# Five edits to a one-core hybrid attention/convolution layer kernel: q's norm factor in the exponential's scale, the side bank in halves, late quarters of q, the gate's division, the first and the last block

## The chip, the cores and the metric

One core of one Trainium2 chip runs the whole layer in one launch. The metric is device time in microseconds. The kernel before was timed three times: 932.99, 933.21 and 934.81 us, median 933.21 us. Lower is better.

## The reference

One sequence of T = 512 tokens, model width D = 2048, one layer. The products are float32, and the kernel must reproduce them closely, which is why it splits each operand (below).

```python
h = rms_norm(x, norm_gain)
z = h @ w_in                                  # 2048 x 6656
q, k, v, g_attn, c_b, c_c, c_h, g_conv = split(z)
q = partial_rope(rms_norm(q, q_norm_gain))    # 16 heads of 64
k = partial_rope(rms_norm(k, k_norm_gain))    # 4 heads of 64
# sliding window of 128, blocks of 128, a learned sink per head
scores = q @ k.T * HEAD_DIM ** -0.5           # masked
m = max(max(scores), sink)
e = exp(scores - m)
probs = e / (sum(e) + exp(sink - m))
y_attn = (probs @ v) * silu(g_attn)
y_conv = c_b * conv3(c_c * c_h) * silu(g_conv)
x = x + concat(y_attn, y_conv) @ w_out
gate = sigmoid(rms_norm(x, ple_gate_norm_gain) @ w_ple_gate + b_ple_gate)
x = x + gate * rms_norm(p @ w_ple_proj, ple_norm_gain)
```

## The kernel before

**Products.** Every float32 operand is split into two parts of a shorter format, a high and a low one (`halves`, L199 a cast on ACT, L200 a subtraction on DVE), and each product is three matmuls: high by high, low by high, high by low. Weights arrive by DMA (`wx`, `wy`, `ws`, `raw`), their parts are `wh` and `wl`; the parts of the activations are `hsh` and `hsl`, and sums of them, used by a seven-product scheme, are called `form`.

**Head.** K and V are projected first, in eight chunks c of two k each (L482 to L504). Inside the loop the next chunk's weights are split, then the next two blocks of x are multiplied by the norm's gain and split (`split_x`, L427 to L431), then some forms are made. For blocks 0 and 1 the split reads x directly (L427, L428), and x itself is rescaled in place right after (L429); from block 2 on, x is rescaled (L431) and then split.

**Groups.** Then come nine groups of 28 steps (`run_step`). A step is twelve matmuls of 128x512 at L241, 2.72 us. Ahead of its matmuls a step makes the weight sums needed four steps on and splits the weight needed two steps on; behind them come the jobs entered with `soon(after, s, ...)`. The split has three buffers, so it cannot run ahead by more than that. Group 0 makes q, in quarters: `qs[t, n]` holds token blocks 2t and 2t+1 of column half n. Quarters (0,1) and (1,1) are joined in steps 17 to 22, (0,0) and (1,0) only at its end. Groups 1 to 8 make the gate of the convolution, the convolution, the gate of the attention (group 4), the output projection (5 and 6) and the gate of the embeddings (7 and 8).

**Norms.** The norm of x is not applied ahead of the projection. Its factor per token, `rx_tok`, and the head norms are applied behind it: `head_sums` squares a quarter (ACT) and sums it per head (DVE L548); `head_rstd` multiplies by the square of the token factor (L552), scales (L300) and raises to the power -1/2 on POOL (L305); `times_token` (L556) multiplies by the token factor again; `scale_q` multiplies q by the result (L579, 128x512 each) and `rope` turns it (L407 to L409). `rb` (L709) is a 128x512 copy of `rx2_tok`, the square of that factor (the profile prints both as rx_tok), which four transposes on PE (L734) turn into rows for K; ACT copies them out of PSUM to `rx` (L735).

**Attention.** It runs beside seven GEMM tiles of the convolution (`gemm_tile`, L700). After every six matmuls of a tile (1.36 us) a tick lets due work in. The sixteen units (four heads of one K/V head, one block of 128 queries) start at tick 13 + 34u//15: `turn_q` three ticks earlier (two transposes of q into the side bank `psm`, L777, evicted into `st` at L781 and L782), then the scores (L790, L791), the mask and the maximum (L796, on DVE, four per unit, result `negm`), the exponentials (L801, ACT), the sums (L805 to L808), the transposes of the probabilities (L816) five ticks after the scores, their split into `pth` and `ptl`, and the product with the values (L826, L827) at seven ticks.

**Group 4.** z, the gate's projection, goes through silu (L992) and is divided by the softmax's sums: `normalise` (L1079) multiplies eight pieces of 128x64 by one column of `rs` each, on ACT, per call. Then it is transposed and multiplied by the attention's output (`times`, L1090).

**Last steps.** The embedding gate's last blocks: `whole` (L1231) adds up z, a sigmoid follows (L1298), then the factor of e (L1246) and x (L1300).

**What sets the order.** On every engine the instructions stand in one queue and start in the order of the queue. PE's order is the order of the code throughout. In the head, in group 0 and in the groups behind the attention the other queues follow the code too; in the attention phase a scheduler orders ACT, DVE and POOL by their readiness, and can put an instruction of the second phase into the end of group 0.

Of the kernel before, what the change touches and what calls it, by code (L numbers as in the profile page):

```python
# [15 lines left out]
P = 128  # L16
# [19 lines left out]
def hymba_layer(ctx: ExitStack, tc: tile.TileContext, io):  # L36
# [177 lines left out]
    def run_step(s, forms):  # L214
# [21 lines left out]
        def products(t, f=f, c=c, wh=wh, wl=wl, first=first, last=last):  # L236
            for i in range(2):
                _, h, l = forms[2 * c + i][f]
                h, l = (a[:, t * P : (t + 1) * P] for a in (h, l))
                for n, (a, w) in enumerate(((h, wh), (l, wh), (h, wl))):  # L240
                    nc.tensor.matmul(  # L241
                        ps[t], a, w[:, i], start=start and first and i == 0 and n == 0,
                        stop=last and i == 1 and n == 2, skip_group_check=not start,
                    )
# [4 lines left out]
        elif s == len(steps) - 1:  # L249
# [4 lines left out]
            products(1)  # L254
# [161 lines left out]
    def split_w(c, i=None):  # L416
        if i is None:
            kv_split.append(new_split())
            halves(*kv_split[c], kv_raw[c])
        else:  # L420
            halves(*(w[:, i] for w in kv_split[c]), kv_raw[c][:, i])

    def split_x(k):
        x, g = xpair[k // 2][:, k % 2], norm_g[:, k : k + 1]
        h, l = (hsp.tile([P, T], F32R, tag="h", name="hs" + n) for n in "hl")
        if k < 2:
            nc.scalar.activation(h, x, AF.Copy, scale=g)  # L427
            stt(l, x, g, f32(h), op0=ALU.mult, op1=ALU.subtract)  # L428
            nc.scalar.activation(x, x, AF.Copy, scale=g)  # L429
        else:  # L430
            nc.scalar.activation(x, x, AF.Copy, scale=g)  # L431
# [46 lines left out]
    kv_split.append(new_split())  # L478
# [3 lines left out]
    for c in range(8):  # L482
        if c > 1:
            form63(c - 2) if c - 2 < 6 else None
        if c < 7:
            split_w(c + 1)
            split_x(2 * c + 2)
            split_x(2 * c + 3)
        else:
            prepare(1)  # L490
        form_sums(c)
# [76 lines left out]
    def finish_q(t, n, junk):  # L568
        ms = small.tile([P, 2, 8], F32, name="msq", bufs=4)
        blocks = slice(2 * t, 2 * t + 2)  # L570
        z = q_of(t, n)

        def squares(b):
            head_sums(z[:, b], ms[:, b], junk("sqq"))

        def scale():
            times_token(ms, tok["x"][:, blocks])
            for b in range(2):
                tt(z[:, b], z[:, b], ms[:, b].unsqueeze(2).broadcast_to([P, 8, HD]), op=ALU.mult)  # L579

        return squares, lambda: head_rstd(ms, rx2_tok[:, blocks]), scale, lambda: rope(z, 0, blocks, mtile)
# [45 lines left out]
    q_then = {}  # L627

    def square_q(t, n, b, junk):
        if b == 0:  # L630
            squares, *q_then[t, n] = finish_q(t, n, junk)
            q_then[t, n].append(squares)
        q_then[t, n][3](b)

    for t in range(2):
        for b in range(2):
            soon(after, 21 + t + b, square_q, t, 1, b, itile)
        soon(after, 23 + t, lambda t=t: q_then[t, 1][0]())
# [30 lines left out]
    ps_m = second.enter_context(tc.tile_pool(name="ps_m", bufs=1, space=PSUM, side="right", reuse_waits="tile"))  # L669

# [798 lines left out]
```

## Time and profile before

| what | value |
| --- | --- |
| median of three runs | 933.21 us |
| the profiled execution's own time | 934.14 us |
| its span | 932.4 us |
| mean granted clock of PE | 0.995 of full speed |
| DVE busy | 731.0 us, 78% |
| ACT busy | 543.2 us, 58% |
| POOL busy | 150.5 us, 16% |
| DMA moved | 189.83 MB, 204 GB/s on average |

An engine's row says how long it had work under way; the waits of an engine say how long it stood still and which engine's result ended that. Of an instruction's row, the first number is its start, the second its duration, and a wait before it stands in brackets with what ended it. Matmuls overlap, so the distance between two starts (0.23 us for 128x512) and not the duration is what one costs.

### The profile page before, as it was taken

The page shows a single profiled execution, that of the slowest core. Times are in us where ns is not written, and L with a number is a line of the kernel's source. Part 1 is how long each engine was busy: PE and PEld are TensorE (multiplying, and loading weights), DVE is VectorE, ACT ScalarE, POOL GpSimd, SP SyncE. Part 2 cuts the span into 40 slices and gives each one's busy share as a digit, 9 for nine tenths or more (in the row PEclk, how much of TensorE's full clock was granted, in tenths as well). Part 3 has the DMA queues.
Part 4 walks back from the last instruction along what each step waited for, and adds up shares of the span by engine and source line. Part 5 has one row for each costly group of instructions (what it writes and reads, how often), then busy time and mean ns, then how long its engine had stood idle before and what let it go on. Part 6 is the DMA issues. An engine that isn't in the chain of part 4 may idle for free.

```text
span 932.4 us, 12106 instructions
## 1 busy us (share of the span) xinstructions
PE 912.5 (98%) x4202; PEld 755.6 (81%) x4202; DVE 731.0 (78%) x1064; ACT 543.2 (58%) x903; POOL 150.5 (16%) x200
## 2 busy tenths in 40 slices
PE   8999999899999999999999999999999999999997
PEld 7888878778888888888888888778888888888885
DVE  5878897888865777776768678878868696999778
ACT  6767856667862443545345357665657566665452
POOL 4232032323231001000100110011120112001100
PEclk9999999999999999999999999999999999999999
DMA  8999536434458768327725988675996895578747
GB/s 296 361 297 313 184 113 231 168 76 91 102 118 271 282 206 225 90 97 224 198 89 169 283 231 243 207 177 166 280 340 176 226 301 136 136 238 270 181 135 214
DMA packets 69085, 189.83 MB, mean 204 GB/s; under 512 B 8096, under 2 KB 14560, under 8 KB 69024
## 3 DMA queue, kind: packets, MB, share of 16 engines
q1 hardware_dynamic: 47520, 131.09, 40.5%
q0 software_dynamic: 21360, 57.96, 28.0%
q8 instruction: 33, 0.54, 0.2%
q14 instruction: 28, 0.23, 0.1%
q10 hardware_dynamic: 144, 0.01, 0.0%
HBM read 159.67 MB, written 29.36 MB: 203 GB/s over the span
## 4 chain that ended last, share of the span: by engine, by line
PE 64%; DVE 3%; ACT 1%; DMA 1%; issue 1%; SPq 0%; DVEq 0%
PE psp L241 57%; PE pst L241 4%; PE pst L986 1%; DMA e<-e 1%; PE pst L1346 1%; PE psg L700 1%; DVE wl L200 1%; ACT z L1079 1%; DVE form L200 0%; DVE wy L189 0%; ACT z L992 0%; DVE raw L1090 0%; ACT wh L199 0%; DVE z L323 0%; ACT form L199 0%
## 5 line engine op out<-in xcount | busy, mean ns | idle before, releaser
L241 PE MATMUL psp<-wh,form 128*128 128x512 f32 x1280 | 396.3, 391 | 2.1 <-ACT wh L199 2.1
L241 PEld LDWEIGHTS psp<-wh,form 128*128 128x128 f32 x1280 | 240.0, 188 | 51.7 <-ACT wh L199 2.5
L241 PE MATMUL psp<-wl,form 128*128 128x512 f32 x640 | 249.8, 390 | 0.0
L200 DVE TENSOR_TENSOR wl<-wy,wh 128x1024 fp32r<-128x1024 f32 x108 | 131.7, 1222 | 54.6 <-ACT wh L199 53.8
L199 ACT CAST wh<-wy 128x1024 fp32r<-128x1024 f32 x108 | 113.3, 1051 | 94.4 <-PE psp L241 70.8
L241 PEld LDWEIGHTS psp<-wl,form 128*128 128x128 f32 x640 | 120.4, 188 | 25.8 <-DVE wl L200 0.8
L200 DVE TENSOR_TENSOR wl<-wx,wh 128x1024 fp32r<-128x1024 f32 x72 | 88.0, 1223 | 51.1 <-ACT wh L199 51.0
L241 PE MATMUL psp<-wl,hsh 128*128 128x512 f32 x304 | 118.7, 390 | 2.0 <-DVE wl L200 2.0
L199 ACT CAST wh<-ws 128x1024 fp32r<-128x1024 f32 x72 | 75.9, 1054 | 74.0 <-PE psp L241 53.3
L241 PE MATMUL psp<-wh,hsh 128*128 128x512 f32 x304 | 118.8, 391 | 0.0
L241 PE MATMUL psp<-wh,hsl 128*128 128x512 f32 x304 | 118.3, 389 | 0.0
L199 ACT CAST wh<-wx 128x1024 fp32r<-128x1024 f32 x72 | 75.7, 1052 | 73.0 <-PE psp L241 51.1
L200 DVE TENSOR_TENSOR wl<-ws,wh 128x1024 fp32r<-128x1024 f32 x72 | 88.1, 1223 | 29.0 <-ACT wh L199 28.8
L189 DVE TENSOR_TENSOR wy<-wy,ws 128x1024 f32<-128x1024 f32 x72 | 87.7, 1218 | 0.0
L241 PEld LDWEIGHTS psp<-wl,hsh 128*128 128x128 f32 x304 | 57.1, 188 | 14.9 <-DVE wl L200 2.9
L241 PEld LDWEIGHTS psp<-wh,hsl 128*128 128x128 f32 x304 | 57.1, 188 | 11.8
L241 PEld LDWEIGHTS psp<-wh,hsh 128*128 128x128 f32 x304 | 57.1, 188 | 11.7 <-ACT wh L199 0.2
L700 PE MATMUL psg<-hsh,wh 128*128 128x512 f32 x112 | 46.7, 417 | 0.0
L200 DVE TENSOR_TENSOR wl<-raw,wh 128x1024 fp32r<-128x1024 f32 (+1 forms) x29 | 34.4, 1187 | 15.2 <-ACT wh L199 15.0
L169 POOL DMA_DIRECT2D wy<-in_w_mid x16 | 14.0, 874 | 199.2 <-DVE wy L189 108.7
L700 PE MATMUL psg<-hsl,wh 128*128 128x512 f32 x112 | 44.2, 395 | 0.0
L700 PE MATMUL psg<-hsh,wl 128*128 128x512 f32 x112 | 44.2, 394 | 0.0
(218 smaller groups left out, 1324.9 us busy)
## 6 DMA issues: line engine op xcount, KB each, us to landing
ws<-in_w_mid SPq DMA_DIRECT2D x40, 512.0 KB, 4.5
wx<-in_w_mid SPq DMA_DIRECT2D x24, 512.0 KB, 3.5
wy<-in_w_mid SPq DMA_DIRECT2D x20, 512.0 KB, 6.1
h<-form POOLq DMA_DIRECT2D x32, 256.0 KB, 5.8
wy<-in_w_mid POOLq DMA_DIRECT2D x16, 512.0 KB, 8.3
raw<-in_w_in SPq DMA_DIRECT2D x16, 512.0 KB, 3.6
wx<-in_w_out SPq DMA_DIRECT2D x16, 512.0 KB, 6.6
ws<-in_w_out SPq DMA_DIRECT2D x16, 512.0 KB, 5.4
```

What stands on the lines that cost most here:

```text
L169: nc.gpsimd.dma_start(t, w[n, r, j, c], accum_op=ALU.add)
L189: tt(y, y, got[g, "s1" if f == 6 else "s0", c], op=ALU.add)
L199: nc.scalar.copy(h, src)
L200: tt(l, src, f32(h), op=ALU.subtract)
L241: nc.tensor.matmul(ps[t], a, w[:, i], start=start and first and i == 0 and n == 0, stop=last and i == 1 and n == 2, skip_group_check=not s ...
L700: nc.tensor.matmul(ps, w[:, k % 8], a, start=k == 0 and n == 0, stop=k == KT - 1 and n == 2)
L986: nc.tensor.transpose(pt[:, b], quads[b // 2][:, b % 2, f * P : (f + 1) * P], ident)
L1079: nc.scalar.activation(z, z, AF.Copy, scale=rs[:, 2 * t + b, 8 * n + i : 8 * n + i + 1])
L1346: nc.tensor.matmul(ps, w[:, k % 8], a, start=k == 0 and n == 0, stop=k == KT - 1 and n == 2)
```

## The change

- **Head.** `split_x` splits blocks 0 to 3 from x directly, and the rescaling of x is its own function, called later in the loop: blocks 0 and 1 behind chunk 0's splits, 2 and 3 behind chunk 1's. Chunk 1's weight is split in two halves, each followed by one block of x, and the very first weight half is cast on DVE.
- **rx's rows.** `rb` and its four transposes move from the attention phase (at tick 2) to behind step 25 of group 0; the copy out of PSUM follows the start of the second phase.
- **q's head norms.** `finish_q` falls into `square_q`, `rstd_q` and `rope_q`. The quarter is no longer multiplied (eight operations of 128x512 go); instead the factor enters the softmax. The maximum is taken over the unscaled scores, two new operations of 128x4 turn it into `negm` (L809, L810), and the exponential reads the factor as its scale. `times_token` now follows `head_rstd` at once. In group 0, `rstd_q` of quarters (0,1) and (1,1) stands behind steps 24 and 25, where `head_rstd` stood behind 23 and 24.
- **Late quarters.** The squares of (0,0) and (1,0) move from ticks 13 and 14 to ticks 19 to 22, their factors from 14 and 15 to 21 and 23, their rope from 19 and 20 to 24 and 26.
- **Side bank.** `psm` is one tile of two halves; `turn_q` takes them in turn, and K's four transposes go two and two.
- **Spacing.** Units start at 13 + 36u//15.
- **Group 4.** `normalise` takes four pieces at a time, at steps 18 to 24, 28 and 29; the first half of quarter (0,0) and the last quarter go through DVE (`normalise_wide`); and these jobs are entered behind those that make the forms.
- **Last step.** Its second half of matmuls goes in two halves of columns (twelve of 128x256 for six of 128x512), and the sigmoid of a piece follows its `whole`.

DVE at the end of group 0, before, between the subtractions for steps 25 and 26 and the copy of `rb` (`msq_1205` and `msq_1233` are the sums of squares of quarters (0,1) and (1,1), `msk` is K's, `ptsl` the low part of the layer's embeddings; `wl_1265` belongs to step 26, `wl_1288` to step 27):

```order
L556 TENSOR_TENSOR msk_715<-msk_715,r_x_1202 128x16
L757 SCALAR_TENSOR_TENSOR vv_1421<-kv_713,r_x_1202,vv_1421 128x4x64
L300 TENSOR_SCALAR msq_1205<-msq_1205 128x16
L548 TENSOR_REDUCE msq_1233<-sqq_1257 128x8
L200 TENSOR_TENSOR wl_1265<-wy_576,wh_1264 128x1024
L552 TENSOR_TENSOR msq_1233<-msq_1233,rx2_tok_716 128x16
L200 TENSOR_TENSOR ptsl_1373<-pt_1262,ptsh_1372 128x1024
L300 TENSOR_SCALAR msq_1233<-msq_1233 128x16
L200 TENSOR_TENSOR wl_1288<-wy_579,wh_1287 128x1024
L323 TENSOR_TENSOR z_786<-z_786,psp_1077 128x1024
L200 TENSOR_TENSOR wl_1317<-raw_1260,wh_1316 128x1024
L709 COPY rb_1376<-rx2_tok_716 128x512
```

The same place after, from `ptsl` on, with the quarters' sums now `msq_1207` and `msq_1235`; `wl_1288` belongs to step 27, and the subtractions for steps 25 and 26 stand ahead of the first row. L570 is `times_token`, which reads what POOL has raised to the power behind L301:

```order
L200 TENSOR_TENSOR ptsl_1385<-pt_1261,ptsh_1384 128x1024
L301 TENSOR_SCALAR msq_1207<-msq_1207 128x16
L570 TENSOR_TENSOR msk_717<-msk_717,r_x_1204 128x16
L765 SCALAR_TENSOR_TENSOR vv_1425<-kv_715,r_x_1204,vv_1425 128x4x64
L570 TENSOR_TENSOR msq_1207<-msq_1207,r_x_1204 128x16
L200 TENSOR_TENSOR wl_1288<-wy_581,wh_1287 128x1024
L566 TENSOR_TENSOR msq_1235<-msq_1235,rx2_tok_718 128x16
L576 TENSOR_TENSOR kv_713<-kv_713,msk_717 128x256
L301 TENSOR_SCALAR msq_1235<-msq_1235 128x16
L576 TENSOR_TENSOR kv_714<-kv_714,msk_717 128x256
L570 TENSOR_TENSOR msq_1235<-msq_1235,r_x_1204 128x16
L650 COPY rb_1307<-rx2_tok_718 128x512
```

Before, nothing in this stretch reads the powers of `msq`; after, two rows do, each behind its own L301, and the second of them is the row ahead of the copy of `rb`.

On PE, the transposes of `rb` stood among the GEMM's matmuls, before:

```order
L700 MATMUL psg_1426<-hsl_263,wh_1316 128x512
L700 MATMUL psg_1426<-hsh_262,wl_1317 128x512
L734 MATMUL psm_1445<-ident_211,rb_1376 128x128 x4
L700 MATMUL psg_1426<-hsh_310,wh_1316 128x512
L700 MATMUL psg_1426<-hsl_311,wh_1316 128x512
L700 MATMUL psg_1426<-hsh_310,wl_1317 128x512
```

and after they stand between the last matmul of step 25 and the first of step 26 of group 0:

```order
L241 MATMUL psp_1079<-wh_1240,hsl_624 128x512
L241 MATMUL psp_1079<-wl_1241,hsh_623 128x512
L653 MATMUL pst_1309<-ident_211,rb_1307 128x128 x4
L241 MATMUL psp_723<-wh_1263,hsh_434 128x512
L241 MATMUL psp_723<-wh_1263,hsl_435 128x512
L241 MATMUL psp_723<-wl_1264,hsh_434 128x512
```

They have moved ahead of 24 matmuls of group 0 and 12 of the GEMM.

On ACT in group 4, from the cast of the weight for step 23 (`wy`), before:

```order
L199 CAST wh_5483<-wy_4818 128x1024
L992 ACTIVATE z_5132<-z_5132,r_x_1202 128x512 x2
L1079 ACTIVATE z_5132<-z_5132,rs_1423 128x64 x8
L199 CAST form_5511<-raw_5328 128x256
L199 CAST form_5514<-g_5479 128x256
L199 CAST wh_5523<-wy_4841 128x1024
L1079 ACTIVATE z_5132<-z_5132,rs_1423 128x64 x8
```

and after:

```order
L199 CAST wh_5490<-wy_4829 128x1024
L199 CAST form_5508<-raw_5339 128x256
L199 CAST form_5511<-g_5482 128x256
L1003 ACTIVATE z_5143<-z_5143,r_x_1204 128x512 x2
L1079 ACTIVATE z_5319<-z_5319,rs_1428 128x64 x4
L199 CAST wh_5526<-wy_4852 128x1024
```

The two forms have moved ahead of the silu and of the division, and four pieces of the division instead of eight stand ahead of the next weight's cast.

The diff, cut to its core:

```diff
@@ run_step
-        def products(t, f=f, c=c, wh=wh, wl=wl, first=first, last=last):
+        def products(t, f=f, c=c, wh=wh, wl=wl, first=first, last=last, cols=slice(0, T)):
...
-            products(1)
+            for half in range(2):
+                products(1, cols=slice(half * 2 * P, (half + 1) * 2 * P))
@@ head
+    def scale_x(k):
+        x = xpair[k // 2][:, k % 2]
+        nc.scalar.activation(x, x, AF.Copy, scale=norm_g[:, k : k + 1])
...
-        if k < 2:
+        if k < 4:
             nc.scalar.activation(h, x, AF.Copy, scale=g)
             stt(l, x, g, f32(h), op0=ALU.mult, op1=ALU.subtract)
-            nc.scalar.activation(x, x, AF.Copy, scale=g)
...
-            split_w(c + 1)
-            split_x(2 * c + 2)
-            split_x(2 * c + 3)
+            if c:
+                split_w(c + 1)
+            for i in range(2):
+                if c == 0:
+                    split_w(1, i)
+                split_x(2 * c + 2 + i)
...
+        if c < 2:
+            for i in range(2):
+                scale_x(2 * c + i)
@@ group 0
+    def rstd_q(t, n):
+        head_rstd(rq[t, n], rx2_tok[:, blocks])
+        times_token(rq[t, n], tok["x"][:, blocks])
...
-        soon(after, 23 + t, lambda t=t: q_then[t, 1][0]())
+        soon(after, 24 + t, rstd_q, t, 1)
+    def rx2_rows():
+        rb = itile("rb").rearrange("p (b t) -> p b t", t=P)
+        nc.vector.tensor_copy(rb, rx2_tok.unsqueeze(2).broadcast_to([P, NB, P]))
+        rows_ps.append(ps_t.tile([P, T], F32, name="pst"))
+        for b in range(NB):
+            nc.tensor.transpose(rows_ps[0][:, b * P : (b + 1) * P], rb[:, b, :], ident)
+
+    soon(after, 25, rx2_rows)
@@ attention phase
+    psm = ps_m.tile([P, 2, 2 * P], F32, name="psm")
...
-            at(13 + t, lambda t=t, b=b: square_q(t, 0, b, mtile))
-        at(14 + t, lambda t=t: q_then[t, 0][0]())
-        at(19 + t, lambda t=t: scale_q(t, 0))
+            at(19 + 2 * t + b, lambda t=t, b=b: square_q(t, 0, b, mtile))
+        at(21 + 2 * t, lambda t=t: rstd_q(t, 0))
+        at(24 + 2 * t, lambda t=t: rope_q(t, 0))
...
-            pt = ps_m.tile([P, T], F32, name="psm")[:, : 2 * P].rearrange("p (f t) -> p f t", t=P)
+            pt = psm[:, turns_done[0] % 2].rearrange("p (f t) -> p f t", t=P)
...
-                    t[:, r, lo:], sc[r // 2][:, r % 2, lo:], mask[:, lo:], -(HD**-0.5), nsink[:, h : h + 1],
-                    ALU.add, ALU.min, negm[:, r : r + 1],
+                    t[:, r, lo:], sc[r // 2][:, r % 2, lo:], mask[:, lo:], HD**-0.5, NEG,
+                    ALU.add, ALU.max, negm[:, r : r + 1],
                 )
+            tt(negm, negm, r_q, op=ALU.mult)
+            stt(negm, negm, -1.0, nsink[:, 4 * j : 4 * j + 4], op0=ALU.mult, op1=ALU.min)
...
-                    t[:, r, lo:], t[:, r, lo:], AF.Exp, scale=-1.0, bias=negm[:, r : r + 1],
+                    t[:, r, lo:], t[:, r, lo:], AF.Exp, scale=r_q[:, r : r + 1], bias=negm[:, r : r + 1],
...
-        attention(j, n, 13 + 34 * u // 15)
+        attention(j, n, 13 + 36 * u // 15)
@@ attn_group
-        soon(after, s0 + 21, lambda: normalise(1, 1, 0))
-        soon(after, s0 + 22, lambda: normalise(1, 1, 1))
...
+        for t, n, b, h, s in (
+            (0, 1, 0, 0, 18), (0, 1, 1, 0, 19), (0, 1, 0, 1, 20), (0, 1, 1, 1, 21),
+            (1, 1, 0, 0, 22), (1, 1, 1, 0, 22), (1, 1, 0, 1, 23), (1, 1, 1, 1, 24), (0, 0, 0, 1, 28), (0, 0, 1, 1, 29),
+        ):
+            soon(after, s0 + s, normalise, t, n, b, h)
@@ gate_group
             for c in cols:
                 whole(1, 0, b, c)
+                nc.scalar.activation(q[1, 0][:, b, c], q[1, 0][:, b, c], AF.Sigmoid)
             for c in cols:
-                piece(1, 0, b, c)
+                piece(1, 0, b, c, True)
```

98 lines of the change are left out of this document (43 added, 55 removed).

## The prediction

> **What bounds the kernel now.** I read the page's row of PE first, then the list of what PE waited for, then its granted clock around the two longest waits.
>
> ```profile
> PE 912.5 (98%) x4202; PEld 755.6 (81%) x4202; DVE 731.0 (78%) x1064; ACT 543.2 (58%) x903; POOL 150.5 (16%) x200
> ```
>
> PE has work under way in 98% of the span, and the change takes almost no matmul away. So it can win only what PE loses by standing still or by a lowered clock, and lose only by making PE stand still elsewhere.
>
> ```profile
> PE psm L777 <- DVE st L782: 2.6, 3, 1.0
> PE pss L790 <- DVE negm L796: 2.5, 1, 2.5
> PE psp L241 <- ACT wh L199: 2.1, 1, 2.1
> PE psp L241 <- DVE wl L200: 2.0, 2, 1.9
> PE psm L740 <- ACT rx L735: 1.4, 1, 1.4
> PE psp L501 <- ACT hsh L199: 1.3, 1, 1.3
> ...
> PE pso L827 <- DVE ptl L200: 0.5, 1, 0.5
> ```
>
> Columns: total us, number, longest. The first, second and last rows belong to the attention phase, the third and fourth to group 4, the fifth to the start of the second phase, the sixth to the head: the edits aim at every one of them. A wait also costs what the clock loses behind it; of three stretches (busy times by engine, then PEclk, then DMA share and GB/s):
>
> ```profile
> 186.00:190.00 4.00, 3.99 (x16) 3.31 (x15) 3.81 (x12) 1.67 (x9) 0.00 (x0) 0.57 0.16 57
> 596.00:600.00 4.00, 3.76 (x15) 2.79 (x16) 4.00 (x7) 3.58 (x5) 0.00 (x0) 1.00 1.02 289
> 613.00:618.00 5.00, 4.96 (x14) 3.58 (x15) 3.37 (x4) 5.00 (x13) 0.00 (x0) 0.67 1.05 271
> ```
>
> Behind the wait of 2.54 us the clock was 0.57 for 4 us, 4 x 0.43 = 1.7 us lost; behind the 2.09 us wait 5 x 0.33 = 1.65 us; behind the 1.87 us wait (the middle row) nothing. So a wait of somewhat over 2 us costs itself and about 1.7 us more.
>
> **The rows of rx, moved into group 0: a new wait.** This is the largest term.
>
> ```profile
> 121.56 0.39 PE L241 MATMUL psp<-wh,hsh 128*128 128x512 f32 x1
> 127.00 0.39 PE L700 MATMUL psg<-hsh,wh 128*128 128x512 f32 x1
> 117.90 1.22 DVE L200 TENSOR_TENSOR wl<-ws,wh 128x1024 fp32r<-128x1024 f32 x1
> 119.67 0.68 DVE L548 TENSOR_REDUCE msq<-sqq 128x8 f32<-128x512 f32 x1
> 122.62 0.17 DVE L300 TENSOR_SCALAR msq<-msq 128x16 f32<-128x16 f32 x1
> 126.10 0.42 DVE L709 COPY rb<-rx_tok 128x512 f32<-128x512 f32 x1
> 119.84 2.90 POOL L305 TENSOR_TENSOR msq<-msq,half_neg 128x16 f32<-128x16 f32 x1 [1.19 <-DVE msq L300]
> 180.53 0.18 DVE L556 TENSOR_TENSOR msq<-msq,r_x 128x16 f32<-128x16 f32 x1 [1.37 <-POOL msq L305]
> ```
>
> Step 26 begins at 121.56, and the 24 matmuls to the GEMM's first at 127.00 take 0.227 us each. So the transposes of `rb` stand in PE's queue at that time, and `rb` stands on DVE behind two products that each wait for a power on POOL, 2.90 us each; that DVE really waits for such a power is seen at 180.53. By the new order and these durations DVE goes: subtraction for step 25 from 117.90, the sum, the subtraction for step 26 to 120.8, L566 and `ptsl` (a subtraction too) to 122.0, L301 to 122.2; power to 125.1; L570; the subtraction for step 27 to 126.3, L566, one K product (128x256, taken like `rb`), L301 to 127.0; power to 129.9; L570; `rb` to 130.5. PE restarts at 130.6 instead of 121.6: **+9.0 us**. Behind the waiting transposes stand steps 26 and 27 and the whole GEMM, so nothing covers it. The clock behind it costs **+1.7 us** like the stretch at 186. Bounds: with the two powers at nothing the wait would be 9.0 - 5.8 = 3.2 us; with one more subtraction (1.1) ahead of `rb` 10.1 us. No moved step issues a DMA, and POOL has nothing else to do at that time.
>
> The Trainium skill ("TensorE: Matmul & The Clock Gate", Part 1) has the clock fall to half after an idle window of about 3.4 us and recover after a busy one. The trace agrees on half speed, but a wait of 2.54 us was already enough, so the trace decides for short waits. By either, the wait of 9 us costs the same.
>
> **What that removes.** The transposes leave the GEMM, and K no longer waits for `rx`:
>
> ```profile
> 132.70 0.39 PE L700 MATMUL psg<-hsh,wl 128*128 128x512 f32 x1
> 134.48 0.66 PE L740 MATMUL psm<-ident,kv 128*128 128x128 f32 x4 [1.40 <-ACT rx L735]
> ```
>
> The next start would have been at 132.93: **-1.55 us**. The four transposes cost the same in both places. K's transposes in two pieces cost nothing while DVE and ACT have had 9 us more to run ahead.
>
> **The head.**
>
> ```profile
> 10.23 1.07 PE L501 MATMUL psp<-wl,hsh 128*128 128x512 f32 x4
> 12.56 1.20 PE L501 MATMUL psp<-wh,hsh 128*128 128x512 f32 x4 [1.26 <-ACT hsh L199]
> 8.84 0.72 ACT L429 ACTIVATE x<-x,norm_gain 128x512 f32<-128x512 f32 x1 [0.82 <-DVE hsl L428]
> 15.19 1.05 ACT L199 CAST wh<-raw 128x1024 fp32r<-128x1024 f32 x1
> 20.73 1.05 ACT L199 CAST wh<-raw 128x1024 fp32r<-128x1024 f32 x1
> ```
>
> Four matmuls take 4 x 0.227 = 0.91 us, so 12.56 could have been 11.14: 1.42 us lost. ACT spends 0.82 us of waiting and 0.72 of work on each of two rescales (the row shows the second) that stand ahead of the casts PE wants; they go behind them. But ACT needs 20.73 - 15.19 = 5.54 us a chunk and PE 24 x 0.227 = 5.45, so ACT has no room for the rescales (four of 0.72 us) that now fall into chunks 0 and 1, and a part comes back at the next chunks. Between nothing and -1.42 I take **-1.0 us**.
>
> **Attention.** Its losses of before: 2.6 + 2.5 + 0.5 + 1.7 (clock) = 7.3 us, and 0.2 for restarts: 7.5. The rows of a unit and of what leaves DVE:
>
> ```profile
> L579 DVE TENSOR_TENSOR z<-z,msq 128x512 f32<-128x512 f32 x8 | 5.3, 686 | 0.0
> 186.11 0.08 DVE L796 DVE_READ_ACCUMULATOR2_ANT negm<- 128x1 f32 x1
> 185.07 0.51 ACT L801 ACTIVATE prob<-prob,negm 128x256 f32<-128x256 f32 x1 [1.69 <-DVE negm L796]
> 186.57 0.49 ACT L801 ACTIVATE prob<-prob,negm 128x256 f32<-128x256 f32 x1
> 174.70 5.80 POOL L305 TENSOR_TENSOR msq<-msq,half_neg 128x16 f32<-128x16 f32 x2 [2.35 <-DVE msq L300]
> ```
>
> Removed: the waits for the side bank (2.6), since one half can be written while the other is evicted; four of the products of L579 from the busiest part (2.7 us of DVE). Added: the first exponential of a unit could start after the first of four maxima (185.07, while the last was read at 186.11); now it waits for all four and two operations of 128x4 (up to 0.17 us each, L300's time for 128x16), so a unit's exponentials end about 1.4 us later. And the late quarters' factors make DVE wait for POOL in the middle of units 1 to 4, now by up to the whole 2.9 us, since L570 follows L301 with nothing but one small row between, where it waited 1.37 us. Behind it stand `ptl` and `st`, for which PE waits. Lower bound: the slack absorbs it all, -7.5. Upper bound: one power (2.9), 1.4 for each of the first five units and one lowered clock: 11.6 lost, +4.1. Following the new order row by row I find waits of 4.1 at units 1 and 2 together (one power, one delay), 1.85 at units 0 and 4, 1.4 at units 3, 5 and 7 and later, and half of a lowered clock, 0.85: 8.2 us, **+0.7 us**. The later spacing costs nothing: the last unit now comes two ticks later, and its values fall ahead of the 48 matmuls at L1346, which don't need them (without these it would be 2.7 us).
>
> **Group 4.**
>
> ```profile
> 588.63 1.34 ACT L992 ACTIVATE z<-z,r_x 128x512 f32<-128x512 f32 x2 [3.05 <-DVE z L323]
> 589.87 2.01 ACT L1079 ACTIVATE z<-z,rs 128x64 f32<-128x64 f32 x8
> 592.20 0.43 DVE L200 TENSOR_TENSOR form<-raw,form 128x256 fp32r<-128x256 f32 x1 [2.47 <-ACT form L199]
> 594.81 1.22 DVE L200 TENSOR_TENSOR wl<-wy,wh 128x1024 fp32r<-128x1024 f32 x1
> 596.08 0.50 PE L241 MATMUL psp<-wl,hsh 128*128 128x512 f32 x1 [1.87 <-DVE wl L200]
> 613.00 1.22 PE L241 MATMUL psp<-wh,form 128*128 128x512 f32 x2 [2.09 <-ACT wh L199]
> ```
>
> ACT stands 3.05 us for the join, then puts silu and eight pieces (2.01 us) ahead of two forms for which DVE stands 2.47 us, and so the `wl` that PE waits 1.87 us for comes at 594.81. At 613 the same pattern costs 2.09 us and the clock. With forms first and four pieces at a time, ACT's stretch ahead of the next cast shrinks by 1 us and DVE's wait goes. The losses are 1.87 + 0.15 + 2.09 + 1.65 and about 0.3 at each of three restarts (a single matmul of 0.50 instead of 0.39 us, and what PE takes to begin again), 6.7; I leave 0.7 for two short waits at the transposes and at step 29: **-6.0 us**, between 0 and -6.7. The eight pieces that go to DVE as two operations stand where DVE has room once the forms no longer hold it.
>
> **Last step.**
>
> ```profile
> 913.11 11.88 DMA e<-e
> 925.08 0.76 DVE z L1246
> ...
> 926.48 0.49 DVE z L1231
> ```
>
> The chain of waits runs through a load of e that lands at 924.99, behind it one DVE queue to the end, in an order the edit leaves as it was. DVE comes to the last block's `whole` at 926.48, behind that load, so earlier columns and an earlier sigmoid wait for DVE: **0**. Twelve half-width matmuls in place of six cost between nothing and six more starts, 1.4 us, of which the load hides about 1; if the load came earlier, up to 0.5 us could be won.
>
> **The sum.** +9.0 + 1.7 - 1.55 - 1.0 + 0.7 - 6.0 + 0 = +2.85 us. On the profiled execution's 934.14 us this is 937.0; that execution lies 0.93 above the median of the three, so I forecast **936.1 us** against 933.21.
>
> **The rivals.**
> (a) *Attention runs clean.* The halves of the side bank and the lighter DVE leave no wait: 936.1 - 8.2 = 927.9 us, faster. For it speaks that three of the five waits there are for the side bank; against it the later exponentials. It decides the sign once the phase loses under about 3 us. Chance 0.18.
> (b) *The wait for `rb` is short.* If the powers cost little, 3.2 us and the clock remain: 930.3 us; if it is hidden altogether, 925.4. For it: spans on POOL are rough, and another power (128x4) took 1.06 us. Against: DVE's wait at 180.53. Chance 0.09.
> (c) *Group 4 gains nothing*, that is, this part does not do what it says: the DMA share there is 1.02 to 1.05, so late loads may set the pace and the waits return under another name: 942 us. Against: both waits name ACT and DVE, not a DMA. Chance 0.10.
> (d) *Attention at its upper bound*, +4.1 instead of +0.7: 939.5 us. Chance 0.15.
> (e) *No clock lost behind waits under 3.4 us*, so that attention comes to 7.35: 935.25 us; the stretch at 186 speaks against it. Chance 0.03. The Trainium skill's rule on the idle window ("TensorE: Matmul & The Clock Gate", Part 1) is of this kind.
> The forecast keeps 0.45, with 933 to 939.5 as its own range.
>
> **How the numbers follow.** A measurement here tells 0.2%, 1.87 us, from no change. Over 935.1 us: 0.32 of the forecast, all of (c) and (d), half of (e): 0.58. Under 931.3: 0.14 of (a), 0.06 of (b): 0.20. Between: 0.22. The range 929 to 941 leaves out most of (c) above, and half of (a) and (b) below.
>
> **What would show it.** Right: a PE wait of 8 to 10 us at the first L653 row, ended by DVE's copy of `rb`, with DVE waiting for POOL at L570 twice; a clock near 0.5 behind it; no row L740 or L777 among PE's waits; no PE wait over 1 us in steps 23 to 29 of group 4; 1 us less before step 0 of group 0. Wrong: the L653 row starting within a few us of step 25's end, or waits in the attention phase under 3 us or over 10.

## The result, and the profile after

The changed kernel takes 948.51 us (median of four, 947.2 to 949.17) against 934.01 us before (four, 932.99 to 935.81): ratio 1.0151, 95% interval 1.0131 to 1.0172. It is slower, as forecast, but by 14.5 us and not by 2.9, and 948.5 lies outside the range of 929 to 941. One of the four executions of a later run, the three parts alone, took 2377.68 us for a reason that stays open; its median of 927.18 us is that of all four, the other three took 925.87 to 927.45 us, and its ratio is theirs. The page and the list of what PE waited for, of the changed kernel:

```profile
span 945.4 us, 12136 instructions
...
PE 914.5 (97%) x4208; PEld 757.5 (80%) x4208; DVE 728.4 (77%) x1091; ACT 548.2 (58%) x897; POOL 152.2 (16%) x200
```

```profile
PE psm L786 <- DVE st L791: 9.3, 4, 3.7
PE pst L653 <- DVE rb L650: 9.2, 1, 9.2
PE psm L749 <- ACT kr L750: 1.7, 2, 1.1
PE pso L838 <- DVE ptl L200: 1.5, 2, 1.3
PE pss L799 <- DVE st L791: 1.2, 1, 1.2
PE pst L364 <- DVE zeros L360: 1.1, 1, 1.1
PE psp L515 <- ACT hsh L437: 0.4, 1, 0.4
```

The two waits of group 4 (L241) are gone, the wait at `rb` is there, and the side bank `psm`, which cost 2.6 us before, now costs 9.3. K's transposes (L749), where the wait for `rx` was to go, wait 1.7 us for `kr`. In the attention phase the waits come to 13.8 us, over the 10 us that the prediction named as a sign of being wrong. Three of the waits are followed by a lowered clock (columns as before, PEclk third from the end):

```profile
131.00:136.00 5.00, 5.00 (x17) 4.00 (x16) 5.00 (x23) 0.29 (x1) 0.20 (x2) 0.60 0.56 175
195.00:200.00 5.00, 3.18 (x9) 2.61 (x10) 2.79 (x9) 3.51 (x12) 1.94 (x1) 0.66 0.09 35
250.00:255.00 5.00, 4.51 (x19) 3.88 (x20) 1.42 (x4) 1.89 (x4) 1.70 (x2) 0.66 0.59 150
```

Three starts on PE cut each span into stages: the first matmul of group 0 (L241), of the GEMM (L700, after: L719), and of the tile behind the attention phase (L1346, after: L1361). The lengths below are the differences of these starts.

| kernel | up to group 0 | group 0 | attention phase | the rest | span |
| --- | --- | --- | --- | --- | --- |
| before | 50.8 | 76.2 | 155.3 | 650.1 | 932.4 |
| after | 50.2 | 88.3 | 163.3 | 643.6 | 945.4 |
| difference | -0.6 | +12.1 | +8.0 | -6.5 | +13.0 |

The forecast by the same stages was -1.0, +10.7, -0.85 (-1.55 and +0.7), -6.0. Group 0 is off by 1.4 us; what is off by much is the attention phase, by 9 us. The spans are of the two profiled executions, 934.14 and 947.20 us, which differ by 1.4 us less than the medians.

### The profile page after: what moved, and what is told of

The parts are those of the page before. It is cut to its first block, busy times and chain, and to the rows that moved or that the text cites. A ratio compares the mean times of both kernels' runs of the same rounds, so it can differ in the third digit from the quotient of the medians.

```text
span 945.4 us, 12136 instructions
## 1 busy us (share of the span) xinstructions
PE 914.5 (97%) x4208; PEld 757.5 (80%) x4208; DVE 728.4 (77%) x1091; ACT 548.2 (58%) x897; POOL 152.2 (16%) x200
## 4 chain that ended last, share of the span: by engine, by line
PE 82%; DVE 7%; ACT 6%; issue 2%; POOL 1%; DMA 1%; SPq 0%; DVEq 0%; ACTq 0%; POOLq 0%
PE psp L241 64%; PE psp L515 4%; PE psg L719 4%; PE pst L241 3%; ACT prob L812 3%; PE pst L997 2%; PE pss L878 1%; DVE wl L200 1%; PE pst L1361 1%; PE pst L878 1%; POOL msq L306 1%; DVE ptl L200 1%; DVE prob L805 1%; DVE st L791 1%; DMA x<-in_x 1%
## 5 line engine op out<-in xcount | busy, mean ns | idle before, releaser
L241 PE MATMUL psp<-wh,form 128*128 128x512 f32 x1280 | 395.4, 390 | 0.0
L241 PEld LDWEIGHTS psp<-wh,form 128*128 128x128 f32 x1280 | 239.3, 188 | 49.1
L241 PE MATMUL psp<-wl,form 128*128 128x512 f32 x640 | 249.3, 390 | 0.0
L241 PEld LDWEIGHTS psp<-wl,form 128*128 128x128 f32 x640 | 120.1, 188 | 25.5 <-DVE wl L200 0.4
L200 DVE TENSOR_TENSOR wl<-wx,wh 128x1024 fp32r<-128x1024 f32 x72 | 88.0, 1223 | 50.8 <-ACT wh L199 50.8
L241 PE MATMUL psp<-wh,hsh 128*128 128x512 f32 x304 | 119.6, 393 | 0.0
L241 PE MATMUL psp<-wh,hsl 128*128 128x512 f32 x304 | 119.0, 392 | 0.0
L241 PE MATMUL psp<-wl,hsh 128*128 128x512 f32 x304 | 119.0, 392 | 0.0
L241 PEld LDWEIGHTS psp<-wl,hsh 128*128 128x128 f32 x304 | 57.5, 189 | 12.2
L241 PEld LDWEIGHTS psp<-wh,hsh 128*128 128x128 f32 x304 | 57.7, 190 | 11.8
L241 PEld LDWEIGHTS psp<-wh,hsl 128*128 128x128 f32 x304 | 57.5, 189 | 11.9
L719 PE MATMUL psg<-hsh,wh 128*128 128x512 f32 x112 | 46.5, 415 | 0.0
L719 PE MATMUL psg<-hsh,wl 128*128 128x512 f32 x112 | 44.8, 400 | 0.0
L719 PE MATMUL psg<-hsl,wh 128*128 128x512 f32 x112 | 44.6, 399 | 0.0
L199 ACT CAST wh<-raw 128x1024 fp32r<-128x1024 f32 (+1 forms) x29 | 29.2, 1008 | 21.9 <-PE psp L241 15.6
```

What stands on the lines that cost most here:

```text
L199: nc.scalar.copy(h, src)
L200: tt(l, src, f32(h), op=ALU.subtract)
L241: nc.tensor.matmul(ps[t][:, cols], a, w[:, i, cols], start=start and first and i == 0 and n == 0, stop=last and i == 1 and n == 2, skip_gr ...
L719: nc.tensor.matmul(ps, w[:, k % 8], a, start=k == 0 and n == 0, stop=k == KT - 1 and n == 2)
```

## The experiments

Times are medians; ratios are against the kernel before on the same chip. That kernel came to 934.01 us beside the changed kernel and to 933.19 to 933.48 beside these runs, so by the ratios a run's gain on the changed kernel comes out 0.6 to 1.8 us smaller than by the medians; with intervals of about 1.5 us either way, a difference of under 2 us between two runs says little. First come two edits undone in the changed kernel, then three parts of the change together, and one part alone, put into the kernel before.

**The rows of rx back at tick 2.**

```diff
-    soon(after, 25, rx2_rows)
...
+    at(2, rx2_rows)
```

> The changed kernel with one edit undone: the rows of rx are copied and transposed at tick 2 again. The trace of the changed kernel has a wait of 9.22 us at these transposes and about 1.75 us of lowered clock behind it. If that is the whole price and the attention phase loses what it loses for reasons of its own (theory: the exponentials), the time falls by 10 to 11.5 us, to about 937.5, and the waits of the attention phase stay at 10 to 14 us. If instead the phase loses because it starts 11 us later against the loads and DVE (rival), its waits fall below 8 us too and the time comes to 931 or less.

Measured: 943.53 us, ratio 1.0108 (1.0091 to 1.0125): 5.0 us less, not 10 to 11.5. The waits of the attention phase stay, each at its place, so the late start is not their cause. But DVE still stands for POOL in group 0, and now two other matmuls pay for it; rows of PE in this run:

```profile
126.02 0.50 PE L241 MATMUL psp<-wl,hsh 128*128 128x512 f32 x1 [1.93 <-DVE wl L200]
...
132.09 0.50 PE L708 MATMUL psg<-hsh,wl 128*128 128x512 f32 x1 [1.46 <-DVE wl L200]
```

Group 0 takes 79.8 us (76.2 before), so the move back wins 8.5 us there; but the phase takes 167.3 us, 3.9 more than in the changed kernel. Of these 1.46 are the second row's, and most of the rest is a third stretch of lowered clock, behind a wait of 1.15 us at 208.28, where the changed kernel has the same wait (at 214.47) and keeps its clock. The window of this run, then of the changed kernel:

```profile
208.00:213.00 5.00, 4.72 (x21) 4.12 (x22) 3.82 (x9) 4.72 (x15) 0.66 (x1) 0.66 0.15 27
```

```profile
214.00:219.00 5.00, 4.53 (x29) 4.05 (x30) 3.82 (x9) 4.92 (x15) 0.67 (x1) 1.00 0.15 27
```

**The side bank taken whole.**

```diff
-            pt = psm[:, turns_done[0] % 2].rearrange("p (f t) -> p f t", t=P)
+            pt = ps_m.tile([P, T], F32, name="psm")[:, : 2 * P].rearrange("p (f t) -> p f t", t=P)
```

> The changed kernel with the side bank taken whole again, one tile per use, K's four transposes in one go. If the halves buy nothing, because PE waits for the evictions of the use just before in either form, the waits at q's transposes stay at 8 to 11 us, the two waits of 1.06 and 0.62 us at K's transposes go, and the time is 0 to 2.5 us lower than that of the changed kernel. If the halves do let PE run ahead (what the prediction took), the waits grow, and the time is 3 us or more above the changed kernel.

Measured: 947.56 us, ratio 1.0147 (1.0131 to 1.0164), 1.0 us below the changed kernel, which is not told from none. PE's waits in this run:

```profile
PE psm L781 <- DVE st L786: 9.1, 4, 3.7
PE pso L833 <- DVE ptl L200: 2.5, 3, 2.1
```

The halves buy nothing: 9.1 us against 9.3, and K's two waits, which only the halves made, are gone (most of that comes back at the values). In the changed kernel's trace each of the four waits ends with the eviction of the use just before, though that use lay in the other half. The halves were one tile here; two tiles apart were not tried.

**Head, group 4 and last step alone, on the kernel before.**

> The kernel before with three parts of the change alone: the head, the division of group 4 in small pieces, the last step in halves. By the stages of the two traces (0.64 us less ahead of group 0, 6.5 us less behind the attention phase) the time is 926 to 928 us against 934.0. If the gain behind the attention phase came from the later start and not from the pieces, it is 932 or more.

The edits are those of the diff in `run_step`, the head, `attn_group` and `gate_group`. Measured: 927.18 us, ratio 0.9928 (0.9911 to 0.9945). The rest behind the attention phase takes 643.7 us, as in the changed kernel: the gain there belongs to the pieces and not to the later start.

**The factor in the exponential's scale alone, on the kernel before.**

```diff
-            for b in range(2):
-                tt(z[:, b], z[:, b], ms[:, b].unsqueeze(2).broadcast_to([P, 8, HD]), op=ALU.mult)
...
+            tt(negm, negm, r_q, op=ALU.mult)
+            stt(negm, negm, -1.0, nsink[:, 4 * j : 4 * j + 4], op0=ALU.mult, op1=ALU.min)
```

> The kernel before with the factor of q's heads in the exponential's scale alone (no products of q, two small operations more a unit), all else at its old place. Theory: the exponentials now wait for all four maxima and hold back the evictions of the side bank that stand behind them on ACT, so the waits at q's transposes and at the scores grow from 5.1 to 9 us or more and the time is 4 to 9 us above that before. Rival (the late quarters' new place or the spacing does it): the time is within 2 us of before, or below it, since 5.3 us of DVE go.

Measured: 933.5 us, ratio 0.9998 (0.9989 to 1.0007). My theory fell: the phase is 153.8 us, 1.5 less than before. The waits at q's transposes do grow,

```profile
PE psm L777 <- DVE st L782: 6.0, 6, 2.1
```

from 2.6 to 6.0 us, but in six short ones, and the waits of 2.5 us at the scores and 1.4 at `rx` are gone. The sum of PE's waits in the phase is what it was, 6.9 us against 7.0; what makes the phase shorter is the lowered clock behind the wait at the scores (1.7 us), which this execution does not have.

Next the spacing and the late quarters, and the sum of what had been harmless.

**The spacing alone, on the kernel before** (36u//15 for 34u//15).

> The kernel before with the units at 13 + 36u//15 instead of 34u//15, nothing else. If the spacing moves turns and evictions against each other so that PE waits for the side bank (theory: spacing), the waits at q's transposes grow from 2.6 to 8 us or more and the time is 5 us or more above before. If it does not matter (theory: late quarters), the time is within 1.5 us of before.

Measured: 932.15 us, ratio 0.9988 (0.9978 to 0.9997); the phase is 153.1 us. The waits at q's transposes are 5.0 us, 2.4 more than before, one of them 3.49; the wait at the scores is gone here too.

**The late quarters back at their old ticks, in the changed kernel.**

> The changed kernel with the late quarters' squares, factors and rope at their old ticks (13 and 14, 14 and 15, 19 and 20). Theory: late quarters. The waits of the attention phase (13.7 us and about 3.5 us of clock in the changed kernel) fall to about those of the factor alone, 4.7 us, and the time from 948 to about 936 to 938. Theory: spacing. The waits at 232.96 and 250.49, which come behind the last rope, stay, and the time falls by 5 us at most.

Measured: 952.88 us, ratio 1.0213 (1.0196 to 1.0231), 4.4 us *longer*: neither theory. With the second token factor still behind the power, DVE's stand for POOL now falls into the first units; of PE in this run:

```profile
195.47 0.58 PE L799 MATMUL pss<-khh,st 128*128 128x256 f32 x1 [4.19 <-DVE st L791]
...
256.45 0.69 PE L786 MATMUL psm<-ident,z 128*128 128x128 f32 x2 [3.66 <-DVE st L791]
```

The wait of 3.66 us stays, so the quarters do not make it.

**The old spacing, in the changed kernel.**

> The changed kernel with the units at 13 + 34u//15 again. Theory: spacing. The waits of 1.39 and 3.66 us at 232.96 and 250.49 go, with the clock behind the second (about 1.8 us), and the time falls by 5 us or more, to 943 or less. Theory: late quarters. Time within 2 us of the changed kernel's.

Measured: 943.37 us, ratio 1.0112 (1.0096 to 1.0127), 5.1 us less; behind 204 us no wait of the phase reaches 1 us. So the spacing matters here and not in the kernel before. One wait of 3.18 us at a turn (203.51) stays.

**Three parts and the factor**, all else as before.

> The kernel before with head, group 4 in small pieces, last step in halves, and the factor in the exponential's scale; no moved rows, quarters, halves or spacing. The parts add: 927.2 us by the three parts alone, less the 1.5 us that the second phase is shorter with the factor alone: 925 to 927 us. If the factor's gain is lost again when the phase starts 0.7 us earlier, 927 to 929.

Measured: 925.85 us, ratio 0.9920 (0.9904 to 0.9937), in the range forecast for parts that add. That the factor wins its 1.5 us here is not shown: the interval overlaps that of the three parts alone, and the phase of the profiled execution is 154.8 us against 154.1 there.

**Factor and spacing, on the kernel before.**

> The kernel before with the factor in the exponential's scale and the spacing 36u//15, each of which alone was within 0.2 per cent of before (933.5 and 932.2 us). Theory: the two together shift the evictions of the side bank behind the later exponentials, so a wait of over 3 us at q's transposes stands near unit 5 as in the changed kernel, and the time is 3 to 7 us above before. Rival: the gains add, since each leaves the phase 1.5 and 2.2 us shorter, and the time is 929.5 to 932; then the changed kernel's wait there needs the late quarters or the start that comes 11 us later.

Measured: 940.5 us, ratio 1.0075 (1.0053 to 1.0097), 7 us slower out of two edits that cost nothing singly. That is at the upper edge of the forecast. Its phase is 163.2 us, the changed kernel's 163.3, in part by chance: the waits come to 11.5 us here (13.8 there), the lowered clock to about 6 (3.4 there). PE in this run:

```profile
183.29 0.66 PE L777 MATMUL psm<-ident,z 128*128 128x128 f32 x2 [2.71 <-DVE st L782]
...
201.16 0.66 PE L777 MATMUL psm<-ident,z 128*128 128x128 f32 x2 [2.94 <-DVE st L782]
...
238.61 0.66 PE L777 MATMUL psm<-ident,z 128*128 128x128 f32 x2 [3.71 <-DVE st L782]
```

Transposes of 0.66 us where 0.41 is usual show the lowered clock behind each. The waits at the bank are 9.4 us in all; with one edit they were 6.0 and 5.0, with neither 2.6. So they grow by little more than the sum of the two. The other waits of the phase are 2.1 us with both edits, 0.9 and 1.4 with one, 4.4 with neither. What comes only with both is a lowered clock behind three long waits, about 6 us; with the factor alone there was none, with the spacing alone one of 1.7. The wait of over 3 us stands at unit 11, as the changed kernel's longest does, and not near unit 5.

**The second token factor apart, in the changed kernel.**

```diff
     def rstd_q(t, n):
         head_rstd(rq[t, n], rx2_tok[:, blocks])
-        times_token(rq[t, n], tok["x"][:, blocks])
+
+    def times_q(t, n):
+        times_token(rq[t, n], tok["x"][:, slice(2 * t, 2 * t + 2)])
...
+        times_q(t, 1)
         rope_q(t, 1)
```

> The changed kernel with the second multiplication by the token factor taken out of rstd_q and put ahead of the rope, as the kernel before had it, so that DVE does not wait for POOL right behind the start of a power. Theory: of the wait of 9.22 us at the transposes of rb 3 to 5 us are left, the wait of 3.03 us of DVE at 201 us and with it waits of PE of 1 to 5 us in units 1 and 2 go: the time falls by 5 to 11 us, to 937 to 943. Rival: the powers cost nothing of their own and DVE has other work to wait for; time within 2 us of the changed kernel's.

Measured: 944.97 us, ratio 1.0120 (1.0102 to 1.0137), 3.5 us less (2.9 by the ratios), short of the 5 expected. The wait at `rb` falls from 9.22 to 5.00 us, as said, but the waits of 1.29 and 1.15 us at 212 and 214 became one of 3.57 with a lowered clock of its own. The phase is 166.1 us, 2.8 more than in the changed kernel: its waits are the same (13.5 us), but the clock loses 1.7, 2.6 and 2.9 us behind three of them (0.66 from 192 to 197, 0.56 from 211 to 217, 0.52 from 248 to 254), 7.2 us against 3.4.

**The late quarters at the change's ticks, on the three parts and the factor.**

> The kernel of the three parts and the factor (925.85 us) with the late quarters' squares, factors and scaling at the change's ticks (19 to 22, 21 and 23, 24 and 26), the second multiplication by the token factor kept with the rope. If moving the quarters is good by itself and only the wait for the power spoiled it, 923 to 925.5 us and no PE wait over 2 us in the phase; if the place is bad by itself (squares of 1.1 us on ACT among the first exponentials), 928 to 932.

Measured: 929.75 us, ratio 0.9961 (0.9946 to 0.9976), 3.9 us above the run without them: the new place is bad by itself. A turn waits 3.35 us at 190.94, with a lowered clock behind it (0.66 from 191 to 196).

**Each maximum by itself, with factor and spacing.**

```diff
+                m_r = negm[:, r : r + 1]
+                tt(m_r, m_r, r_q[:, r : r + 1], op=ALU.mult)
+                stt(m_r, m_r, -1.0, nsink[:, 4 * j + r : 4 * j + r + 1], op0=ALU.mult, op1=ALU.min)
...
-            tt(negm, negm, r_q, op=ALU.mult)
-            stt(negm, negm, -1.0, nsink[:, 4 * j : 4 * j + 4], op0=ALU.mult, op1=ALU.min)
```

> As the run with factor and spacing, but each maximum is multiplied and compared by itself right behind it (eight operations of 128x1 a unit instead of two of 128x4), so that the first exponential need not wait for all four. If the later start of the exponentials is what makes the wait near unit 5, that wait falls below 1 us and the time is 3 us or more below the run with factor and spacing; if not, the 96 further small operations on DVE make it 0 to 4 us longer.

Measured: 935.61 us, ratio 1.0022 (1.0013 to 1.0032), 4.9 us below the run with factor and spacing though DVE does 96 more operations. The wait at 201 is gone, the one at 183 grew from 2.71 to 5.22 us, the one at 238 fell from 3.71 to 2.19. So the waits at the bank went from 9.4 to 7.4 us, less evenly than expected, but the time fell as the theory said: the later start of the exponentials is a part of the cause.

**The side bank freed by one copy, in the changed kernel.**

```diff
+            qc = mtile("qc")[:, : 2 * P].rearrange("p (f t) -> p f t", t=P)
+            nc.scalar.copy(qc, pt)
...
-                nc.scalar.copy(st[own, :, hf], pt[own])
-                tt(st[oth, :, hf], pt[own], f32(st[own, :, hf]), op=ALU.subtract)
+                nc.scalar.copy(st[own, :, hf], qc[own])
+                tt(st[oth, :, hf], qc[own], f32(st[own, :, hf]), op=ALU.subtract)
```

> The changed kernel, with q's transposes first copied out of the side bank by one ACT operation and split from that copy, so that the bank is free after one operation instead of four that alternate between ACT and DVE. Theory: the side bank's slow eviction, its second half behind four exponentials on ACT, is what the phase waits for. Then the waits of 9.3 us at q's transposes fall below 3 us, the clock behind them (about 3.5 us) comes back, and the time falls by 7 to 12 us, to 936 to 941. Rival (the phase waits for the exponentials themselves, and the bank only shows it first): the waits move to the scores or the values, and the time stays within 4 us of 948.

Measured: 943.12 us, ratio 1.0112 (1.0097 to 1.0127), 5.4 us less (3.6 by the ratios), between the two forecasts. PE's waits, and then a row of DVE, in this run:

```profile
PE pso L840 <- DVE ptl L200: 5.9, 6, 2.8
...
PE psm L786 <- ACT qc L788: 0.5, 1, 0.5
```

```profile
216.38 0.17 DVE L570 TENSOR_TENSOR msq<-msq,r_x 128x16 f32<-128x16 f32 x1 [2.82 <-POOL msq L306]
```

The waits for the bank go from 9.3 to 0.5 us, so the eviction was what PE waited for; 4.4 us more than in the changed kernel then appear at the values, the longest (2.76 us, at 220.27) behind DVE's stand for the power of a late quarter.

**All of it mended**: freed bank, token factor apart, rows of rx behind step 24 ahead of the factors.

> The run with the freed bank, and besides the rows of rx copied behind step 24 ahead of the factors, and the second token factor with the rope. Theory: the wait at the rows (9.22 us) and its clock go too; 923 to 930 us, the size of the three harmless parts. If more than 3 us of waits are left at the rows, 932 or more.

Measured: 932.24 us, ratio 0.9993 (0.9983 to 1.0003). The wait at the rows is 2.24 us, group 0 takes 79.1; 5.5 us of waits at the values are left. The expected 923 to 930 was missed: the late quarters, the spacing and K's halves were still in it.

**Three parts, the factor and the freed bank.**

> The kernel of the three parts and the factor (925.85 us), with the side bank freed by one copy. It has 6.0 us of waits at q's transposes. Theory: they go almost whole, 920 to 922.5 us. Rival: the sixteen more operations on ACT (0.4 us each) delay the exponentials and what follows them, 924 to 928.

Measured: 924.07 us, ratio 0.9907 (0.9892 to 0.9921), the fastest of all, 24 us below the changed kernel. The waits at the bank are gone,

```profile
PE pss L806 <- DVE negm L812: 2.8, 2, 2.6
PE pso L845 <- DVE ptl L200: 1.6, 5, 0.5
```

but one of 2.6 us at the scores takes a part of their place: the gain on the run without the freed bank is 1.8 us, not 3.5 to 6, and the intervals of the two overlap. So in that kernel the gain of freeing the bank is not shown clear of noise.

## Why the prediction was wrong, step by step

**The rows of rx: right.** The forecast was a restart at 130.6 behind two powers, and a wait of 9.0 us. The changed kernel, DVE first:

```profile
124.81 0.18 DVE L570 TENSOR_TENSOR msq<-msq,r_x 128x16 f32<-128x16 f32 x1 [2.79 <-POOL msq L306]
...
129.75 0.17 DVE L570 TENSOR_TENSOR msq<-msq,r_x 128x16 f32<-128x16 f32 x1 [2.79 <-POOL msq L306]
129.84 0.42 DVE L650 COPY rb<-rx_tok 128x512 f32<-128x512 f32 x1
...
130.32 1.12 PE L653 MATMUL pst<-ident,rb 128*128 128x128 f32 x4 [9.22 <-DVE rb L650]
```

The clock behind it costs 5 x 0.40 = 2.0 us against 1.7, and the transposes themselves run at half clock: 12.1 us for the stage. Undoing the move gives back 8.5 us in group 0, but 3.9 are lost again in the attention phase, which leaves 4.6 by these stages and 5.0 by the medians. The token factor right behind the power keeps DVE standing in either place: with it apart, the wait at `rb` fell to 5.00 us, and with the rows ahead of the factors too to 2.24.

**Group 4 and last step: right; head: not told from chance.** Behind the attention phase the kernel is 6.5 us shorter, against -6.0 and 0; from the start of the last matmul to the end of the span it was 6.7 us before and is 6.4 now, so the last step's part is about 0. Ahead of group 0 it is -0.6 against -1.0. But of kernels with an unchanged head, group 0 began at 50.2 (factor and spacing) to 52.7 us (spacing alone), so -0.6 is within what an unchanged head does. The three parts made alone win 6.1 us.

**Attention: the step that failed.** I put "the waits for the side bank (2.6), since one half can be written while the other is evicted" on the side of what is removed, "the later spacing costs nothing", 8.2 us of loss as the sum and 11.6 as its upper bound. Measured, the phase waits 13.8 us and loses 3.4 more behind the waits at 196.82 and 250.49 (5 x 0.34 each): 17.2 us. Four things were wrong.

First, the halves are not free of each other. The same wait with the bank taken whole (9.1 us) shows that they free nothing. The Trainium skill ("PSUM — Partial Sum Buffer", section "PSUM bank collisions raise a hardware error") says that TensorE and another engine must not touch one bank in the same partitions at the same time, disjoint columns included; the program's waits keep to that. It spoke against this edit, and I had not weighed it. K's two waits (1.06 and 0.62 us) are the halves' own price. The prediction had K's transposes in two pieces at nothing; their 1.7 us undo the 1.55 that it took off for `rx`.

Second, the exponentials. They wait for all four maxima, as forecast, but each is also longer; groups of the changed kernel, then of the kernel before:

```profile
L812 ACT ACTIVATE prob<-prob,negm,msq 128x256 f32<-128x256 f32 x48 | 28.3, 591 | 2.0 <-DVE negm L810 1.8
```

```profile
L801 ACT ACTIVATE prob<-prob,negm 128x256 f32<-128x256 f32 x48 | 23.9, 500 | 7.5 <-DVE negm L796 7.5
```

Four exponentials take 0.36 us more. The Trainium skill ("ScalarE: Activation LUTs", section "What ACT_TABLE_LOAD costs") gives about 93 ns for each operand of 128x1; the trace agrees with 91.

Third, what stands behind them. The longest turn of the changed kernel, from PE, ACT and DVE:

```profile
242.78 0.38 PE L786 MATMUL psm<-ident,z 128*128 128x128 f32 x2
...
245.33 0.37 ACT L790 CAST st<-psm 64x256 fp32r<-64x256 f32 x1
...
246.20 0.15 DVE L809 TENSOR_TENSOR negm<-negm,msq 128x4 f32<-128x4 f32 x1
...
247.03 0.60 ACT L812 ACTIVATE prob<-prob,negm,msq 128x256 f32<-128x256 f32 x1 [0.27 <-DVE negm L810]
...
249.59 0.37 ACT L790 CAST st<-psm 64x256 fp32r<-64x256 f32 x1
...
250.00 0.43 DVE L791 TENSOR_TENSOR st<-psm,st 64x256 fp32r<-64x256 f32 x1
...
250.49 0.44 PE L786 MATMUL psm<-ident,z 128*128 128x128 f32 x2 [3.66 <-DVE st L791]
```

The eviction is four operations that alternate between ACT and DVE. Its second cast stands on ACT behind the four exponentials of the unit before, which wait for the small operations, and so the bank is free 7.7 us after its transposes. Of these, 2.55 us pass before the first cast, a weight's cast takes 1.1 between the two, and the exponentials with their row sums take the stretch from 247.03 to 249.5.

Fourth, the spacing. With the factor at the old spacing a short distance from one turn to the next, without the wait, is 4.5 us (184.43 to 189.81 less the wait of 0.88, in the run with the factor alone), and the eviction is done 5.2 us after the turn there, so the waits stay under 1 us. One turn there comes after 4.1 us, behind an eviction of 6.1, and waits 2.12. At 36u//15 the short distances with a wait are 3.6 to 4.1 us (the last from 230.84 to 238.61 less 3.71, in the run with both), and the evictions that they meet there take 6 to 8 us. In that run this makes waits of 2.7 to 3.7 us, each with a lowered clock. Neither edit costs time alone. The freed bank and the exponentials that start earlier each take 4 to 5 us of it back, which fits this chain. Where the scheduler puts the second cast was readable in the new order; I followed the values' operands there and took the bank as free.

**The rivals.** None held: (a) counted on clean halves, and (d), attention at 11.6 us, was no bound, as it had no term for the bank. (b) and (c) did not come: the wait at `rb` is 9.22 us, and both waits of group 4 are gone. (e) is refuted again by the clock behind the wait of 3.14 us at 196.82. The sign would have come out without the attention phase too (-0.6 + 12.1 - 6.5 = +5.0); the size would not.

**Open.** When the wait at `rb` is shortened (rows back; token factor apart), the phase gets 3 to 4 us longer, in the first run by a wait of 1.46 us, and otherwise for the most part by lowered clock. Why the clock falls behind one of two equal waits no run here shows. How much of the late quarters' 3.9 us is ACT's squares and how much DVE's sums was not tried.

## What to carry to other kernels

An upper bound counts only the resources that one has put into it: for each shared buffer that a change touches, follow who must evict it, in which queue, behind what. Two edits that each move a wait by a microsecond can meet in one place; when both are to be kept, they are timed together. Where a buffer is emptied by operations that alternate between two engines, one copy that empties it first is worth a trial: it took the waits for the bank from 9.3 to 0.5 us here, though part of that came back at the next wait.

## What the runs showed of the hardware

The prediction took it that a wait of somewhat over 2 us costs about 1.7 us of clock besides. The clock does not fall behind every wait of the same length. A wait of 2.54 us was followed by a clock of 0.66 over 5 us (before, from 185), one of 2.56 us by the full clock (the three parts alone, from 185). A wait of 2.12 us was followed by 0.66 (the three parts and the factor) and by 1.00 (the factor alone), both from 177:

```profile
177.00:182.00 5.00, 5.00 (x21) 4.32 (x22) 4.91 (x19) 3.86 (x13) 2.38 (x3) 0.66 0.14 52
```

```profile
177.00:182.00 5.00, 4.87 (x28) 4.25 (x29) 4.89 (x19) 4.35 (x14) 2.62 (x3) 1.00 0.10 39
```

Even a wait of 1.15 us came out both ways (rows back; the changed kernel). The first row behind a wait does not settle it: behind the 3.35 us of the late quarters the transposes took the usual 0.41 us, and 0.7 us later the matmuls went from 0.40 to 0.63. So in these runs a wait of 1 to 3.5 us has to be priced with and without a lowered clock, which cost 1.7 us in most cases and up to 3.1 (0.56 over 7 us, from 201 with factor and spacing). Executions of one kernel differ by as much: beside the last runs the kernel before took 931.68 to 934.66 us, at mean clocks of 0.993 to 0.999.

The maximum, now with constants in place of an operand of 128x1 and as a maximum instead of a minimum, got shorter, 0.418 us against 0.479 for 128x256 on DVE.
